# Sums of squares of the norms: two rounded parts in place of one fp32 product

## The chip, the cores and the metric

The kernel runs on one core of one Trainium2 chip. The metric is the device time of one execution in microseconds (us); lower is better. A core has five engines that run their own instruction queues and meet at semaphores: PE (TensorE, matmuls, with its weight loads shown apart as PEld), DVE (VectorE), ACT (ScalarE), POOL (GpSimd) and SP (SyncE, which issues most DMAs). Matmuls read operands from SBUF and write PSUM; POOL reads and writes SBUF alone.

## The reference

Three blocks follow each other on 512 tokens of width 1024: layer 0 (16 meta tokens are put in front, so 528 rows; a gated linear recurrence "hgrn2" with 4 heads beside latent attention "mla" with 4 heads, then an MLP), layer 1 (a pooling mixer and an MLP), and a second block (sparse attention with 8 heads, a gated linear attention "gla" with 4 heads, then a mixture of 32 experts). What the change touches are norms inside the first and the last of them:

```python
def rmsnorm(x, g):
    xf = x.astype(jnp.float32)
    y = xf * lax.rsqrt(jnp.mean(xf * xf, axis=-1, keepdims=True) + EPS)
    return (y * g.astype(jnp.float32)).astype(x.dtype)

# layer 0: per head of the recurrence (128 wide), per latent (256 wide), per key (192 wide)
o = rmsnorm(o, out_gain) * jax.nn.silu(hg...)
q = jnp.einsum('blr,re->ble', rmsnorm(cq, qa_g), w_q_up)...
kv = jnp.einsum('blr,re->ble', rmsnorm(ckv, kva_g), w_kv_up)...
k = rope_tail(rmsnorm(k, kn_g), cos, sin)
# second block: queries and keys per head of 64, gla output per head of 128
qa = rmsnorm_2(qa.reshape(bsz, s_len, A_HEADS, A_HEAD_DIM), q_norm_g[l])
ka = rmsnorm_2(ka.reshape(bsz, s_len, A_HEADS, A_HEAD_DIM), k_norm_g[l])
o_b = rmsnorm_2(o_b, gla_out_norm_g[l])...
```

## The kernel before

The state is kept transposed: features lie on the 128 partitions, tokens along the free axis, so the residual `h` is eight tiles of 128 x 528 (512 in the second block). Every dense product is made exact enough by splitting both operands into a rounded high part and the remainder (type fp32r) and multiplying three times: high x high, high x low, low x high (`dense`, L289; `mm3`, L266 to L268). ACT rounds (L259) and DVE subtracts (L260); SP streams the raw weights in half megabyte pieces (L253).

A norm over features is a sum over partitions. `ones_sum` (L478) makes it on PE: a constant matrix (`self.ones`, or `self.blk` with two blocks of 64) is the stationary operand, the tile of squares is streamed, both as plain fp32, and every row of the result holds the sum. In layer 0 a result of 528 columns is two halves of 264 in a pair of PSUM banks (L485); in the second block it is one product of 512 columns (L489). `rstd_rows` (L472) then takes Ln (L475) and Exp (L476) on ACT, and DVE multiplies. The squares come from ACT (Square) right before: L810 for a head of the recurrence, L848 for a latent, L942 with an addition at L943 for a key, L1973 for a gla head, L2005 for an attention projection. A latent is 256 wide, two tiles, so its sum has two operands in `pairs`.

Scratch tiles of 528 columns come from a ring of ten places (`tmp`, pool `t`); the second block has a ring of seven places of 512 columns besides (`gtmp`, pool `b2t`). A tile holds its place until its last reader is done, and places go to tiles in the program's order.

The order of the work is written as weaves: generators (`hgrn_head`, `mla_up`, `dsa_proj`, `gla_heads` and others) that yield between pieces are interleaved by `WEAVES` in layer 0 and `WEAVES_2` in the second block. On top of that a planner orders each engine's queue by readiness, with the program's order as priority. In layer 0 the first weave ends with the second latent (`B1`) and its norm; then PSUM is divided anew (`banks(2, 4)`), a mask is loaded through POOL (L634) and the second weave begins with the first head (L569). In the second block the first weave makes the eight attention projections (`dsa_proj`) beside the index products (`index_tile`, Relu at L1820, six scratch places held by their operands); each projection's sum is called behind the next projection's Square, the last one's at the end. Top-k runs on DVE (L1836, L1837) pinned to the program's order. `gla_gate` (L1863) loads a small weight `w2` through POOL (L1867) into a tile of its own and multiplies it at L1873; `rel_bias` fills the ring of seven with its tables and uses them at L1759 and L1774.

## Time and profile before

| | us |
|---|---|
| median of 3 runs | 1750.56 |
| lowest, highest | 1749.06, 1750.74 |
| the profiled execution | 1750.7 |
| its span, first to last instruction | 1748.8 |
| busy: PE, DVE, ACT, POOL | 1700.9, 1090.7, 860.5, 54.5 |
| mean granted clock of PE, share of full speed | 0.987 |

The page gives, for one execution, busy time by engine, the chain of work that ended last, and groups of instructions. Matmuls are pipelined and their ends are modelled, so that records of PE overlap: the mean duration of a record is longer than the step from one to the next, and the chain in order of time is where the step is seen. A releaser behind "<-" is the instruction that ended a wait.

### The profile page before, as it was taken

The numbers are of one execution on the slowest core, as the hardware profiler recorded it, in microseconds if no ns is written. First come the engines' busy times: TensorE is split into PE (matmuls) and PEld (weight loads), VectorE is DVE, ScalarE is ACT, GpSimd is POOL, SyncE is SP. The second block draws the span as 40 slices with busy tenths as digits, with TensorE's granted clock in tenths as the row PEclk, the third lists the DMA queues.
The fourth block names the chain that finished last, engine by engine and source line by source line (L and its number), as shares of the span: only waits on it lengthen the run. The fifth ranks groups of instructions, "written<-read, shape, count | busy, mean of one in ns | idle before, by whom it ended". The sixth has DMA issues, their size and how long they took to land.

```text
span 1748.8 us, 26901 instructions
## 1 busy us (share of the span) xinstructions
PE 1700.9 (97%) x10674; PEld 1494.4 (85%) x10674; DVE 1090.7 (62%) x1885; ACT 860.5 (49%) x1419; POOL 54.5 (3%) x66
## 2 busy tenths in 40 slices
PE   8999999999999999999999999999999999999996
PEld 7999999999999999878888888767767788888884
DVE  7677675643434344553434345589867768999996
ACT  5456654432323133541413134454346359999995
POOL 0000000000000000000000000100000000101111
PEclk9999999999999999999999999999989999999999
DMA  5211113332323232133333334322201468999994
GB/s 190 70 50 49 37 37 106 85 96 86 94 88 94 89 91 79 61 91 93 94 97 96 96 97 135 111 73 73 73 13 55 160 224 292 348 339 377 374 375 136
DMA packets 72482, 228.42 MB, mean 131 GB/s; under 512 B 8456, under 2 KB 8512, under 8 KB 72352
## 3 DMA queue, kind: packets, MB, share of 16 engines
q1 hardware_dynamic: 69120, 216.22, 36.4%
q0 software_dynamic: 3232, 10.44, 3.0%
q8 instruction: 85, 1.39, 0.3%
q14 instruction: 45, 0.37, 0.1%
HBM read 213.50 MB, written 13.12 MB: 130 GB/s over the span
## 4 chain that ended last, share of the span: by engine, by line
PE 92%; DVE 5%; ACT 2%; issue 1%; DMA 0%; SPq 0%; POOL 0%; POOLq 0%; DVEq 0%; ACTq 0%
PE pm L289 32%; PE ps L289 29%; PE ps L1591 7%; PE ps L1571 3%; PE ps L266 3%; PE ps L267 2%; PE ps L268 2%; PE ps L557 2%; PE ps L2062 1%; DVE wlo L260 1%; PE ps L2037 1%; PE ps L1192 1%; PE pm L485 1%; PE ps L2055 1%; DVE acc L1837 1%
## 5 line engine op out<-in xcount | busy, mean ns | idle before, releaser
L259 ACT CAST whi<-wraw 128x1024 fp32r<-128x1024 f32 (+1 forms) x309 | 321.3, 1045 | 606.6 <-PE pm L289 293.1
L260 DVE TENSOR_TENSOR wlo<-wraw,whi 128x1024 fp32r<-128x1024 f32 (+1 forms) x309 | 373.4, 1217 | 42.5 <-ACT whi L259 32.3
L289 PE MATMUL pm<-xh,whi 128*128 128x264 f32 x976 | 202.2, 288 | 8.7 <-ACT whi L259 5.9
L289 PE MATMUL pm<-xh,wlo 128*128 128x264 f32 x976 | 200.9, 287 | 0.5 <-DVE wlo L260 0.5
L289 PE MATMUL pm<-xl,whi 128*128 128x264 f32 x976 | 200.6, 287 | 0.0
L289 PE MATMUL ps<-xh,whi 128*128 128x512 f32 x472 | 192.1, 407 | 0.0
L289 PE MATMUL ps<-xh,wlo 128*128 128x512 f32 x472 | 186.2, 395 | 0.0
L289 PE MATMUL ps<-xl,whi 128*128 128x512 f32 x472 | 185.5, 393 | 0.0
L289 PEld LDWEIGHTS pm<-xh,whi 128*128 128x128 f32 x976 | 152.8, 190 | 9.8 <-ACT whi L259 5.9
L289 PEld LDWEIGHTS pm<-xh,wlo 128*128 128x128 f32 x976 | 152.7, 190 | 0.8 <-DVE wlo L260 0.7
L289 PEld LDWEIGHTS pm<-xl,whi 128*128 128x128 f32 x976 | 152.2, 189 | 0.4 <-DVE xl L467 0.3
L289 PEld LDWEIGHTS ps<-xh,whi 128*128 128x128 f32 x472 | 89.3, 189 | 23.6 <-issue 1.8
L289 PEld LDWEIGHTS ps<-xh,wlo 128*128 128x128 f32 x472 | 89.1, 189 | 21.0
L289 PEld LDWEIGHTS ps<-xl,whi 128*128 128x128 f32 x472 | 89.3, 189 | 19.4 <-issue 0.5
L1591 PE MATMUL ps<-wlo,xg 128*128 128x512 f32 x256 | 103.8, 406 | 1.7 <-DVE wlo L260 1.6
L289 PE MATMUL pm<-ah,whi 128*128 128x264 f32 x512 | 104.2, 285 | 0.0
L289 PE MATMUL pm<-ah,wlo 128*128 128x264 f32 x512 | 104.0, 285 | 0.0
L1591 PE MATMUL ps<-whi,xg 128*128 128x512 f32 x256 | 103.7, 405 | 0.0
L289 PE MATMUL pm<-al,whi 128*128 128x264 f32 x512 | 103.7, 284 | 0.0
L289 PE MATMUL ps<-ah,whi 128*128 128x512 f32 x256 | 101.1, 395 | 0.0
L289 PE MATMUL ps<-ah,wlo 128*128 128x512 f32 x256 | 101.0, 394 | 0.0
L289 PE MATMUL ps<-al,whi 128*128 128x512 f32 x256 | 100.5, 393 | 0.0
(501 smaller groups left out, 3202.4 us busy)
## 6 DMA issues: line engine op xcount, KB each, us to landing
wraw<-in_stream_dram SPq DMA_DIRECT2D x306, 512.0 KB, 3.6
t<-in_stream_dram SPq DMA_DIRECT2D x90, 256.0 KB, 6.9
h<-in_stream_dram SPq DMA_DIRECT2D x37, 512.0 KB, 6.0
h<-in_xT_dram SPq DMA_DIRECT2D x16, 264.0 KB, 4.3
hd<-h SPq DMA_DIRECT2D x8, 256.0 KB, 2.0
h<-hd SPq DMA_DIRECT2D x8, 256.0 KB, 4.2
out_dram<-t SPq DMA_DIRECT2D x8, 256.0 KB, 2.3
gt<-rbd POOLq DMA_DIRECT2D x4, 256.0 KB, 5.6
```

The source lines that it names most:

```text
L259: self.nc.scalar.copy(hi, src)
L260: i = self.nc.vector.tensor_sub(lo, src, hi.bitcast(F32))
L266: nc.tensor.matmul(ps, wh, xh, start=start, stop=False)
L267: nc.tensor.matmul(ps, wh, xl, start=False, stop=False)
L268: nc.tensor.matmul(ps, wl, xh, start=False, stop=stop)
L289: nc.tensor.matmul(ps, w[:, b, :], x[:, sl], start=(first and f and i == 0), stop=(last and l and i == nb - 1))
L485: nc.tensor.matmul(pm[:, s, :H2], l, r[:, s * H2:(s + 1) * H2], start=i == 0, stop=i == len(pairs) - 1)
L557: nc.tensor.matmul(pa[:, j * 64:(j + 1) * 64], xs, self.second(xs, i), start=True, stop=True)
L1192: nc.tensor.matmul(ps[:, i * 128:i * 128 + n], self.z[:, i, cols], self.bands[i][:, g, :n], start=False, stop=i == NT - 1, skip_group_chec ...
L1571: nc.tensor.matmul(pg[:, j * m:(j + 1) * m], src[2 * i + k // 4][:, sl], oh[:, i, :m], start=i == 0, stop=i == NT - 1, skip_group_check=True)
L1591: nc.tensor.matmul(pa, xk, v[:, k], start=kk == 0 and n == 0, stop=kk == 7 and n == 1, skip_group_check=True)
L1837: nc.vector.match_replace(out=acc, in_to_replace=m8, in_values=acc, imm_value=sel)
```

## The change

`ones_sum` takes one constant and a tuple of operands. A new helper `parts` makes that tuple: ACT copies the squares into a rounded tile, POOL subtracts it from the squares for the remainder. The constants `ones` and `blk` are copied once into a rounded tile `c2` by DVE. All sums that go through `ones_sum` are then two rounded products of the same constant. For a latent, POOL first adds the two tiles of squares, so that its sum has one tile too. The gate's weight `w2` moves from a tile of its own into the ring of seven. The sums that use one column of `self.ones` (L427, L926) stay as they are.

```diff
--- before.py
+++ after.py
@@ -475,9 +475,17 @@
         nc.scalar.activation(out, ps, AF.Ln, scale=1.0 / dim, bias=self.epsb)
         nc.scalar.activation(out, out, AF.Exp, scale=-0.5)
 
-    def ones_sum(self, pairs, n=T):
-
-        nc = self.nc
+    def parts(self, x, n=T):
+
+        hi, lo = (self.p_t.tile([128, T], F32R, name="t")[:, :n] for _ in range(2))
+        self.nc.scalar.copy(hi, x)
+        self.nc.gpsimd.tensor_sub(lo, x, hi.bitcast(F32))
+        return hi, lo
+
+    def ones_sum(self, l, x, n=T):
+
+        nc = self.nc
+        pairs = [(l, r) for r in x]
         if n == T:
             pm = self.pm()
             for s in range(2):
@@ -583,6 +591,9 @@
 
         xh, xl = self.xsplit(h, "mix0", first=first)
         nc.sync.dma_start(self.c128, self.a["c128"].rearrange("p (a b) -> p a b", a=4))
+        c2 = self.p_c.tile([128, 2, 128], F32R, name="c2")
+        nc.vector.tensor_copy(c2, self.c128[:, 1:3])
+        self.onesr, self.blkr = c2[:, 0], c2[:, 1]
         self.rb2 = None
         self.o = h
         with ExitStack() as es:
@@ -808,9 +819,10 @@
 
         sq = self.tmp()
         nc.scalar.activation(sq, o, AF.Square)
+        sq = self.parts(sq)
         yield
         yield
-        pn = self.ones_sum([(self.ones, sq)])
+        pn = self.ones_sum(self.onesr, sq)
         ro = self.tmp()
         self.rstd_rows(self.v2(ro), pn, 128)
         while "g" not in st:
@@ -828,7 +840,7 @@
         lat = [([], []), ([], [])]
 
         def norm(which, gname):
-            pn = self.ones_sum([(self.ones, sqs[which, 0]), (self.ones, sqs[which, 1])])
+            pn = self.ones_sum(self.onesr, sqs[which, 2])
             r = self.tmp()
             self.rstd_rows(self.v2(r), pn, 256)
             for j in range(2):
@@ -848,6 +860,8 @@
             nc.scalar.activation(sq, z, AF.Square)
             zs[which, j], sqs[which, j] = z, sq
             if j == 1:
+                nc.gpsimd.tensor_add(sq, sq, sqs[which, 0])
+                sqs[which, 2] = self.parts(sq)
                 return lambda: norm(which, gname)
 
         def keys(pm):
@@ -944,8 +958,10 @@
             krr[h] = p1.tile([128, T], F32, name=("lh00", "lh01", "ll00", "ll01")[h])
             nc.gpsimd.memset(krr[h], 0.0)
 
+            sn = self.parts(sn)
+
             def norm():
-                pn = self.ones_sum([(self.ones, sn)])
+                pn = self.ones_sum(self.onesr, sn)
                 f = self.tmp()
                 self.rstd_rows(self.v2(f), pn, 192)
                 nc.vector.scalar_tensor_tensor(k, k, gg, f, op0=OP.mult, op1=OP.mult)
@@ -1863,7 +1879,7 @@
     def gla_gate(self, p, comb):
 
         nc = self.nc
-        w2 = p.tile([64, 256], F32, name="w2")
+        w2 = self.gtmp(256)
         nc.gpsimd.dma_start(w2[32:48], self.a["gate_w2"])
         gb = p.tile([128, 2], F32, name="gb")
         nc.gpsimd.dma_start(gb, self.a["gate_b"])
@@ -1971,12 +1987,12 @@
             nc.scalar.copy(o, pos[par])
             sq = self.gtmp(S)
             nc.scalar.activation(sq, o, AF.Square)
-            os.append((o, sq))
+            os.append((o, self.parts(sq, S)))
         yield
         for par in range(2):
             h = 2 * f + par
             o, sq = os[par]
-            pn = self.ones_sum([(self.ones, sq)], S)
+            pn = self.ones_sum(self.onesr, sq, S)
             ro = self.gtmp(S)
             n = 0
             while "g" not in gate[h]:
@@ -2003,11 +2019,12 @@
                 nc.vector.tensor_mul(z, pm, rb)
                 sq = self.tmp(S)
                 nc.scalar.activation(sq, z, AF.Square)
+                sq = self.parts(sq, S)
                 if late:
                     late()
 
                 def late(z=z, sq=sq, g=g):
-                    pn = self.ones_sum([(self.blk, sq)], S)
+                    pn = self.ones_sum(self.blkr, sq, S)
                     r = self.tmp(S)
                     self.rstd_rows(r, pn, 64)
                     nc.vector.scalar_tensor_tensor(z, z, g, r, op0=OP.mult, op1=OP.mult)
```

## Rows read from the trace of the kernel before

**Rows 1.** The page: its first line and section 4, the chain by engine.

```profile
span 1748.8 us, 26901 instructions
PE 92%; DVE 5%; ACT 2%; issue 1%; DMA 0%; SPq 0%; POOL 0%; POOLq 0%; DVEq 0%; ACTq 0%
```

**Rows 2.** Groups on PE: line, shapes, count, busy us, mean ns, idle before.

```profile
L485 PE MATMUL pm<-t,c 128*128 128x264 f32 x48 | 12.5, 391 | 1.0 <-ACT t L848 1.0
L489 PE MATMUL ps<-t,c 128*128 128x512 f32 x16 | 8.3, 598 | 0.6 <-ACT t L2005 0.6
L489 PE MATMUL ps<-gt,c 128*128 128x512 f32 x8 | 3.9, 592 | 0.0
```

**Rows 3.** The chain in order of time: start us, length us, what, count.

```profile
52.69 1.78 PE pm L485 x8
231.95 2.94 PE pm L289 x24
1384.86 1.72 PE ps L489 x4
1389.60 5.55 PE ps L289 x24
```

**Rows 4.** Groups on ACT, POOL and DVE (columns as in rows 2).

```profile
L259 ACT CAST lh<-t 128x528 fp32r<-128x528 f32 x4 | 2.4, 628 | 0.8 <-DVE t L836 0.8
L945 POOL MEMSET ll<- 128x528 f32 x2 | 1.1, 536 | 9.5 <-PE pm L289 9.5
L635 DVE CAST msk<-t 128x384 uint8<-128x384 f32 x1 | 0.4, 358 | 0.0
```

**Rows 5.** Timeline, 64 to 68 us: start, length, instruction, idle before and its releaser.

```profile
64.00 0.64 ACT L848 ACTIVATE t<-t 128x528 f32<-128x528 f32 x1
66.34 0.70 ACT L475 ACTIVATE t<-pm,epsb 128x528 f32<-128x528 f32 x1 [1.69 <-PE pm L485]
64.70 1.60 PE L485 MATMUL pm<-t,c 128*128 128x264 f32 x6 [1.03 <-ACT t L848]
67.09 1.16 PE L569 MATMUL ps<-q,kk 128*128 128x128 f32 x8 [0.79 <-ACT t L475]
```

**Rows 6.** Stretches: busy us (instructions) of PE, PEld, DVE, ACT, POOL; PE clock; DMA.

```profile
120.00:140.00 20.00, 20.00 (x123) 17.25 (x122) 11.05 (x19) 15.42 (x29) 0.20 (x1) 1.00 0.15 48
180.00:190.00 10.00, 8.41 (x66) 7.70 (x65) 6.30 (x19) 7.32 (x18) 0.20 (x1) 1.00 0.17 55
1115.00:1182.00 67.00, 66.41 (x286) 44.32 (x286) 52.76 (x112) 35.91 (x63) 3.43 (x5) 1.00 0.28 87
```

**Rows 7.** The chain by line, 1176 to 1211 us.

```profile
by line: DVE acc L1837 26.6%; DVE m L1836 22.7%; DVE wlo L260 12.9%; issue 9.6%; DVE gt L534 4.0%; DVE gt L535 4.0%; DVE gb L1883 3.4%; DVE gt L1880 3.4%; DVE dqa L2013 2.1%; DVE gt L1881 2.1%; DVE dka L2013 1.9%; ACT t L476 1.8%; DVE gt L1
```

**Rows 8.** Timeline of ACT and PE around one attention projection's sum.

```profile
1127.33 0.63 ACT L2005 ACTIVATE t<-dka 128x512 f32<-128x512 f32 x1
1134.42 1.02 PE L489 MATMUL ps<-t,c 128*128 128x512 f32 x2
```

**Rows 9.** The views of single lines: duration ns min/median/max, first and last start us.

```profile
L1759 PE MATMUL ps<-gt,rbt x2: 481/482/484, 1112.1 to 1112.5; 32*8 32x384 f32 x2
L1774 PE MATMUL ps<-gt x8: 592/593/593, 1176.2 to 1179.2; 128*128 128x512 f32 x8
L1867 POOL DMA_DIRECT2D w<-in_gate_w_dram x1: 505/505/505, 1096.2 to 1096.2; - x1
L1873 PE MATMUL ps<-comb,w x4: 587/588/692, 1179.7 to 1181.1; 16*128 16x512 f32 x4
```

**Rows 10.** Timeline of POOL, the mask's load.

```profile
54.63 0.60 POOL L634 DMA_DIRECT2D t<-in_msk_dram  x1 [51.62 <-PE pm L485]
```

**Rows 11.** Timeline of POOL and DVE, 1488 to 1492 us.

```profile
1488.63 2.25 POOL L1496 DMA_INDIRECT out_dram<-y,sr  x1 [16.79 <-ACT xg L1573]
1489.80 1.22 DVE L260 TENSOR_TENSOR wlo<-h,whi 128x1024 fp32r<-128x1024 f32 x1 [0.35 <-ACT whi L259]
1491.14 1.21 DVE L260 TENSOR_TENSOR wlo<-wraw,whi 128x1024 fp32r<-128x1024 f32 x1
```

## Prediction

> **What bounds the kernel now.** I read the views in this order: the page's chain of work, the groups of the sums of squares on the matrix engine, the same sums in the chain in order of time, and then a timeline wherever a sum's inputs come from just ahead of it.
>
> The chain that ended last is PE for 92% of the span [rows 1]. So what PE executes counts one to one wherever PE is packed, and what ACT, DVE or POOL execute counts only where PE, or what PE feeds, waits for it. The sums to be changed are three groups: 48 matmul records of 264 columns at L485 and 16 + 8 records of 512 columns at L489 [rows 2]. An fp32 product leaves two records, so these are 24 products in ten sums (four heads, four keys, two latents with two squares each), two halves a sum, and 12 products in twelve sums of block 2 (eight attention projections, four gated heads).
>
> The mean duration of a record is not its price, since matmuls overlap. The chain in order of time has the price: eight fp32 records in 1.78 us, 0.2225 each, and four of 512 columns in 1.72 us, 0.43 each. The projections around them multiply rounded (fp32r) operands: 24 records of 264 columns in 2.94 us, 0.1225 each, and 24 of 512 in 5.55 us, 0.231 each [rows 3]. A rounded record costs a little over half of an fp32 record, and a rounded product is one record where an fp32 product is two.
>
> **The change part by part.**
>
> Removed from PE: 48 x 0.2225 = 10.7 us and 24 x 0.43 = 10.3 us, together 21.0. Added: every sum is now two rounded products (high and low part) of full width, and the latents' two squares are added first, so ten sums x 2 halves x 2 = 40 x 0.1225 = 4.9 us, and twelve x 2 = 24 x 0.231 = 5.5 us. Net 10.6 us off PE, if every sum stood where PE is packed.
>
> Added ahead of each sum: one ACT copy that rounds (a row of the same shape: 0.63 us) and one POOL subtraction; for each latent norm a POOL addition besides. That is 22 copies (13.9 us of ACT) and 24 POOL operations. The trace has no POOL operation that reads tiles. Its nearest row is a POOL memset of the same 128x528: 0.536 us for one stream written [rows 4]. Three streams, overlapped or one behind the other, lie between 0.54 and 1.6 us; nothing below, since an operation is added and none goes. I take the middle, 1.1 us, and keep both ends. The Trainium skill (GPSIMD Engine Reference, section Elementwise — side-by-side cycle accounting) gives 4497 ns for an addition over 2048 columns, from which 528 columns would be an estimated 1.16 us; by it the latents' term below grows by 0.1 us.
>
> So a sum's inputs come about 0.63 + 1.1 + two hand-overs of 0.06 (Square's end at 64.64 to the matmul at 64.70 [rows 5]) = 1.85 us later, and some sums give up what they gain.
>
> *The second latent's norm.* It is the last thing of the first weave. Its Square ends at 64.64, PE waits for it, six records run, Ln starts at 66.34, and the next PE work (L569) waits for that Ln before it starts at 67.09 [rows 5]; DVE's and PE's next stage stand behind that. From Square to Ln now: 1.70 us. After: 1.1 (add) + 0.63 (copy) + 1.1 (subtract) + 4 x 0.06 + 4 x 0.1225 + 0.31 (last record to Ln, as now: 1.64 - 6 x 0.2225) = 3.87 us. The stage starts 2.2 us later, and the 1.29 us that this sum's records were credited with above are not gained: a loss of 3.5 us against the credit. With POOL's ends it is 2.4 to 4.5; it is 0 if PE finds projection work to do meanwhile, which it did not find in the 0.79 us ahead of L569.
>
> *A head's norm at 185 us.* PE is busy only 8.41 of the 10 us around it, ACT 7.32 [rows 6]. The 0.4 us that the sum saves fills idle time, and the 0.63 us copy queues on ACT ahead of the softmax exponentials that this stretch waits for. Loss 0.7, between 0.4 and 1.0.
>
> *The last two attention sums, 1173.6 to 1176.* From 1176 to 1211 the chain is DVE's top-k steps (L1836, L1837: 49%) [rows 7], so the 0.8 us that PE saves in these two sums returns nothing. The last sum's chain grows, but top-k steps of two blocks are at hand to fill DVE; a POOL subtraction that held DVE up would cost up to 1.1 there. I take 0.8 + 0.5, between 0.8 and 2.4.
>
> *The other sums* I take as covered. In the attention stretch a Square ends at 1127.96 and its sum starts at 1134.42 [rows 8]: 6.5 us of projection matmuls cover 1.85. Among the keys, 120 to 140 us, PE is busy 20.0 of 20 [rows 6], with the values' matmuls as cover; ACT's 15.4 us there grow by about five copies, 3.2 us, and stay under 20. If that cover were gone, a key would cost 1.85 less the 0.4 saved.
>
> *Edits with one answer.* The copy of two constant blocks is one DVE instruction of 256 columns; a conversion of 384 takes 0.36 us [rows 4]. The first sum comes at 52 us, so it lies beside other work: 0, or 0.36 on DVE's path to the first matmul. The gate's weight moves into a ring of seven buffers. Six others and the one-hot table fill the ring, so its load, issued at 1096.2 now, waits for the table's release after L1759, read at 1112; on POOL's queue the bias store and loads follow it. It is read at 1179.7 [rows 9], so some 65 us cover it: 0. Only if it got the buffers that L1774 reads until 1179 would PE wait some 4 us.
>
> The sum: 10.6 - 3.5 - 0.7 - 1.3 = 5.1 us. The profiled execution took 1750.7 us around a span of 1748.8, which is also the runs' median (1750.56) within 0.2. Forecast: 1745.6 us.
>
> **The rivals.**
>
> *All of it returns.* PE has other work at the latents' end, and the chains are covered: 1750.7 - 10.6 = 1740.1. For it: the planner may order PE's work anew. Against: the two waits in rows 5.
>
> *The buffers run out.* The ring of scratch tiles has ten places, and each sum now takes two more of them until it has run. The ring is short already: the mask's load on POOL, ready from the start, waited 51.6 us, until the first latent's sum gave a place back [rows 10]. In the attention projections six of the ten places hold the index operands; the high and low parts hold two more through the following projection, so the index products' Relu and the next Square would wait for places. If each of the eight projections lost 0.6 us of the 1.85 to this, that is 5 us: 1750.5, no change.
>
> *POOL holds DVE up.* Slower. If a POOL operation that reads two tiles keeps a DVE operation with two tile inputs waiting to its end, DVE loses up to 24 x 1.1 = 26 us, where it is busy 52.8 of 67 us [rows 6], and it makes the low halves of the weights that PE needs. Half of that on the path is 13 us, less the 0.5 already taken: 1745.6 + 12.5 = 1758. It decides from 0.2 us an operation (5.1 / 24). Against it, as far as rows go: beside POOL's 2.25 us scatter a DVE subtraction took 1.22 us, and right after it one of the same shape 1.21 [rows 11]; but that POOL instruction reads no tile to compute. The Trainium skill (SBUF — State Buffer, section SBUF: two separate sides) says just this, that the two engines share a pair of ports under an exclusive lock, and that a DVE operation with two inputs in SBUF and a GpSimd operation that reads SBUF block each other for a whole instruction. By that rule this rival's mechanism is certain and only its share on the path is open; no row here has the pair, so the trace neither agrees nor differs.
>
> *It does not do what it says.* The rounded products with the new constant run at the fp32 record's price: 40 x 0.2225 + 24 x 0.43 = 19.2, only 1.8 us off, and the delays of about 4 us remain (2.2, 0.7 and 1.3): some 1753. Against it: all rounded rows show the lower price.
>
> **How the numbers follow.** 0.2%, or 3.5 us, is about what a measurement of this kernel can tell from no change; faster ends at 1747.1, slower begins at 1754.1. The forecast case has 0.50, with a range of its own of 1743 to 1748.5 (the bounds of its terms): 0.41 faster, 0.09 the same. All of it returns: 0.14, faster. Buffers run out: 0.16, the same. POOL holds DVE up: 0.15, slower. Not what it says: 0.05, the same. So faster 0.55, same 0.30, slower 0.15. The range reaches from the full gain to the fp32-priced case, 1740 to 1753; it leaves out the slower rival and little else.
>
> **What would show it.** Right: 40 records at L485's successor at about 0.12 us in the chain and 24 at 0.23; POOL subtractions near 1.1 us; L569's start some 2 us later against the end of the B1 projection; heads, keys and attention sums without a wait ahead of them on PE. Wrong: DVE instructions of unchanged shape that last longer, or start late, beside POOL's; Relu or Square in the attention stretch waiting for a sum.

## The result and the profile after

| | before | after |
|---|---|---|
| median, us | 1749.8 | 1777.6 |
| lowest, highest, us | 1748.2, 1750.7 | 1777.2, 1779.0 |
| the profiled execution, its span, us | 1750.7, 1748.8 | 1777.3, 1775.6 |
| PE's mean granted clock | 0.987 | 0.978 |

The changed kernel takes 1.0161 times the time of the kernel before (95% interval 1.0144 to 1.0179): 28 us more, where 5 less were forecast and the range ended at 1753. The page's chain of the changed kernel breaks off at its last instruction, an output transfer on POOL, so nothing here rests on it. Its groups by line, which answer [rows 2, 4] (columns as there; L493 and L497 are the sums, L481 the rounding copy, L482 the subtraction, L863 the addition of a latent's squares):

```profile
L493 PE MATMUL pm<-t,c 128*128 128x264 f32 x40 | 10.3, 355 | 14.9 <-POOL t L482 6.5 <-ACT t L481 5.1 <-DVE ll L968 3.3
L497 PE MATMUL ps<-t,c 128*128 128x512 f32 x24 | 10.1, 480 | 6.4 <-ACT t L481 4.5 <-POOL t L482 1.9
L481 ACT CAST t<-t 128x528 fp32r<-128x528 f32 x10 | 6.3, 634 | 4.5 <-POOL t L863 3.7 <-DVE t L957 0.6
L481 ACT CAST t<-t 128x512 fp32r<-128x512 f32 x8 | 5.0, 621 | 0.3
L482 POOL TENSOR_TENSOR t<-t 128x528 fp32r<-128x528 f32 x10 | 15.5, 1550 | 77.8 <-ACT t L481 72.1 <-PE ps L268 3.4 <-issue 2.3
L482 POOL TENSOR_TENSOR t<-t 128x512 fp32r<-128x512 f32 x8 | 10.3, 1290 | 46.6 <-ACT t L481 40.2 <-DVE wlo L260 6.4
L863 POOL TENSOR_TENSOR t<-t 128x528 f32<-128x528 f32 x2 | 3.5, 1760 | 59.4 <-ACT t L860 59.4
```

The counts are the forecast ones, 40 and 24 records. What was not forecast stands behind the second bar: PE is idle 14.9 and 6.4 us ahead of its sums, where it was 1.0 and 0.6 before [rows 2].

Where the time went is read by taking the same PE instruction in both traces, by its first start, and subtracting. Lines are those of the kernel before; the first column is its time there, the others how much later (us) the same work starts. The other kernels are those of the experiments.

| place (line before) | before | after | sub_on_dve | keys_as_before | parts_unread | layer0_only | block2_only |
|---|---|---|---|---|---|---|---|
| behind the latents (L569) | 67.1 | 5.0 | 1.5 | 4.7 | 0.3 | 4.8 | 0.0 |
| sums of the queries (L926) | 106.5 | 7.6 | 4.5 | 7.5 | 0.2 | 6.3 | 0.1 |
| behind the keys (L1020) | 143.9 | 17.5 | 12.2 | 8.2 | 2.5 | 18.1 | 0.0 |
| behind the second head's norm (L1066) | 208.9 | 21.0 | 12.7 | 11.2 | 3.4 | 20.2 | 0.1 |
| second block begins (L1799) | 1111.8 | 20.8 | 13.7 | 11.2 | 3.7 | 21.0 | 1.2 |
| last attention sums (L1774) | 1176.2 | 23.0 | 13.5 | 13.4 | 7.9 | 21.1 | 4.0 |
| attention begins (L2037) | 1206.8 | 25.7 | 16.2 | 15.8 | 9.9 | 21.1 | 6.7 |
| behind the gated heads (L1369) | 1442.5 | 26.9 | 14.0 | 16.0 | 9.7 | 21.3 | 7.5 |

So four places lose: the latents (7.6 until PE runs evenly again), the keys (9.9), the norm of the recurrence's second head, at 185 us in the kernel before (3.5), and the end of the attention projections (4.9). The gated heads add 1.2. In `parts_unread` and `layer0_only` some 1.5 us of the row "behind the keys" are not the keys': there the clock fell behind a pause near 112 us (119 in `layer0_only`), ahead of the keys' sums, and in the changed kernel it did not (last section).

*The latents.* Timeline of the changed kernel, which answers [rows 5] (start, length, instruction, idle before and its releaser):

```profile
65.49 0.65 ACT L860 ACTIVATE t<-t 128x528 f32<-128x528 f32 x1
66.21 1.75 POOL L863 TENSOR_TENSOR t<-t 128x528 f32<-128x528 f32 x1 [10.71 <-ACT t L860]
66.72 1.78 DVE L755 TENSOR_TENSOR t<-c,b 128x512 f32<-128x512 f32 x1
67.99 0.63 ACT L481 CAST t<-t 128x528 fp32r<-128x528 f32 x1 [1.86 <-POOL t L863]
68.67 0.59 PE L493 MATMUL pm<-t,c 128*128 128x264 f32 x1 [3.97 <-ACT t L481]
68.70 1.48 POOL L482 TENSOR_TENSOR t<-t 128x528 fp32r<-128x528 f32 x1 [0.74 <-ACT t L481]
68.91 1.56 DVE L543 TENSOR_TENSOR t<-b 128x264 f32<-128x264 f32 x1
70.24 1.03 PE L493 MATMUL pm<-t,c 128*128 128x264 f32 x3 [0.97 <-POOL t L482]
71.30 0.70 ACT L475 ACTIVATE t<-pm,epsb 128x528 f32<-128x528 f32 x1 [2.68 <-PE pm L493]
72.05 2.08 PE L577 MATMUL ps<-q,kk 128*128 128x128 f32 x8 [0.79 <-ACT t L475]
```

From Square's end to Ln it is 71.30 - 66.14 = 5.16 us instead of 1.70. PE waits 3.97 and 0.97 us, and its next work (L577, L569 before) takes 2.08 us where it took 1.16 [rows 5]: the clock has fallen.

*The clock.* Stretches of the changed kernel, columns as in [rows 6]; the last four figures are POOL, PE's granted clock, DMA share, GB/s:

```profile
66.00:78.00 12.00, 7.56 (x32) 6.95 (x33) 8.45 (x13) 4.25 (x8) 3.76 (x3) 0.57 0.18 60
148.00:160.00 12.00, 7.27 (x34) 6.90 (x33) 7.23 (x15) 5.86 (x11) 2.25 (x1) 0.57 0.28 89
203.00:212.00 9.00, 7.95 (x40) 7.54 (x40) 3.38 (x13) 4.16 (x12) 0.10 (x1) 0.62 0.01 2
1196.00:1206.00 10.00, 7.44 (x12) 3.38 (x13) 6.55 (x16) 5.82 (x10) 1.28 (x1) 0.66 0.17 52
```

In each of the four places the clock falls to 0.5, the 1.2 GHz level, after PE has waited. The kernel before ran these places at 1.00. By the means, PE lost 7.56 x 0.43 + 7.27 x 0.43 + 7.95 x 0.38 + 7.44 x 0.34 = 11.9 us there, an estimate, since a mean covers the pauses too. It is on the high side: at the latents it gives 3.3, and what PE falls behind there after the norm is 2.6 (5.0 to 7.6).

So of the 27 us by which the span grew, the idle time ahead of the sums is 19.7 (21.3 less 1.6) and the clock some 12, less the 10.6 of saved work; the 6 that are left are not divided further; other pauses are among them, such as 2.6 us at the softmax beside the second head's norm, where it was 1.4.

*The keys.* The changed kernel's timeline of ACT and POOL for the third and fourth key, with one line of DVE (a weight's subtraction) and one of PE (the fourth key's sum); L956 is a key's Square, L475 Ln:

```profile
142.90 0.70 ACT L475 ACTIVATE t<-pm,epsb 128x528 f32<-128x528 f32 x1 [0.47 <-PE pm L493]
143.50 0.64 ACT L956 ACTIVATE t<-kn 128x528 f32<-128x528 f32 x1
145.04 0.64 ACT L481 CAST t<-t 128x528 fp32r<-128x528 f32 x1
145.76 1.72 POOL L482 TENSOR_TENSOR t<-t 128x528 fp32r<-128x528 f32 x1 [3.65 <-ACT t L481]
148.22 0.70 ACT L475 ACTIVATE t<-pm,epsb 128x528 f32<-128x528 f32 x1 [1.12 <-PE pm L493]
148.81 0.63 ACT L956 ACTIVATE t<-kn 128x528 f32<-128x528 f32 x1
150.81 0.63 ACT L481 CAST t<-t 128x528 fp32r<-128x528 f32 x1
151.40 1.21 DVE L260 TENSOR_TENSOR wlo<-wraw,whi 128x1024 fp32r<-128x1024 f32 x1
151.50 0.59 PE L493 MATMUL pm<-t,c 128*128 128x264 f32 x1 [3.32 <-DVE ll L968]
151.52 2.25 POOL L482 TENSOR_TENSOR t<-t 128x528 fp32r<-128x528 f32 x1 [4.04 <-ACT t L481]
154.89 0.70 ACT L475 ACTIVATE t<-pm,epsb 128x528 f32<-128x528 f32 x1 [3.44 <-PE pm L493]
```

On ACT a key's Square stands behind the Ln of the key before. So copy, subtraction and sum lie in a loop from key to key: 5.3 and 6.7 us from Ln to Ln. Before, the same order of ACT's queue gave 130.83, 134.11 and 137.39, 3.3 us each. How much of the loss is this loop is asked by `square_first` below.

*The second head's norm.* Timeline of POOL, DVE and PE in the changed kernel (L509 multiplies two tiles in SBUF, L1001 is the maximum that the softmax waits for, L1027 the next attention scores), then the same multiplication and scores in the kernel before:

```profile
201.42 1.68 POOL L482 TENSOR_TENSOR t<-t 128x528 fp32r<-128x528 f32 x1 [2.25 <-issue]
201.86 1.80 DVE L509 TENSOR_TENSOR q<-t 128x528 f32<-128x528 f32 x1
203.66 0.41 DVE L1001 TENSOR_REDUCE mx<-pm 128x1 f32<-128x272 f32 x1
205.03 0.82 PE L1027 MATMUL pm<-kn,qn 128*128 128x136 f32 x2 [1.01 <-ACT t L1007]
```

```profile
184.49 0.70 DVE L501 TENSOR_TENSOR q<-t 128x528 f32<-128x528 f32 x1
186.55 0.50 PE L1011 MATMUL pm<-kn,qn 128*128 128x136 f32 x2 [0.18 <-ACT t L991]
```

Beside POOL's subtraction the multiplication takes 1.80 us instead of 0.70; the maximum behind it on DVE comes later, so do the softmax and PE, which waits 1.01 us instead of 0.18. An earlier pause (1.59 instead of 1.22) has the copy in ACT's queue ahead of the softmax. Then the clock falls. With the subtraction on DVE (`sub_on_dve`) the multiplication takes 0.71, the second pause is 0.39, the clock stays at 1.00 and the place loses 0.5 us instead of 3.5.

*The attention projections.* Timeline of the changed kernel around one of them (L2021 Square, L1836 an index product's Relu, L476 the Exp of the norm before, L2030 its multiplication on DVE):

```profile
1148.17 0.63 ACT L2021 ACTIVATE t<-dka 128x512 f32<-128x512 f32 x1
1148.84 0.62 ACT L481 CAST t<-t 128x512 fp32r<-128x512 f32 x1
1149.37 0.68 ACT L475 ACTIVATE t<-ps,epsb 128x512 f32<-128x512 f32 x1
1149.60 1.30 POOL L482 TENSOR_TENSOR t<-t 128x512 fp32r<-128x512 f32 x1 [5.33 <-ACT t L481]
1150.93 0.38 ACT L1836 ACTIVATE t<-ps 128x256 f32<-128x256 f32 x1 [0.88 <-POOL t L482]
1151.21 0.62 ACT L476 ACTIVATE t<-t 128x512 f32<-128x512 f32 x1
1151.87 0.75 DVE L2030 SCALAR_TENSOR_TENSOR dqa<-dqa,qg,t 128x512 f32<-128x512 f32 x1
```

The Relu waits until POOL has read the squares: it needs their place in the ring. Exp stands behind the Relu, and behind Exp the DVE work that comes ahead of the next projection's multiplication. How far that multiplication (L2003 before) starts behind the sum that PE runs at the projection's end, second to eighth projection, in us:

| kernel | 2 | 3 | 4 | 5 | 6 | 7 | 8 |
|---|---|---|---|---|---|---|---|
| before | 0.2 | 0.2 | 0.2 | 0.2 | 0.2 | 0.2 | 0.2 |
| after | 0.2 | 0.2 | 1.6 | 2.9 | 3.7 | 4.2 | 4.2 |
| block2_only | 0.2 | 0.5 | 1.3 | 2.6 | 3.4 | 4.1 | 4.2 |
| parts_unread | 0.2 | 0.2 | 1.2 | 2.1 | 2.5 | 3.0 | 3.4 |
| block2_copy_on_pool | 0.2 | 0.7 | 1.4 | 3.2 | 4.2 | 5.3 | 4.1 |
| block2_relu_psum | 0.2 | 0.2 | 0.6 | 1.1 | 1.8 | 2.3 | 2.6 |
| block2_both | 0.2 | 0.2 | 0.4 | 0.5 | 0.5 | 0.6 | 1.0 |

While projections follow, PE has other work and the lag costs nothing. Behind the last one it has none: it waits 4.45 us for the last sum (1194.10 to 1198.56), and the fourth stretch at half clock follows.

### The profile page after: what moved, and what is told of

It reads as the page before. It is cut to its first block, busy times and chain, and to the rows that moved or that the text cites. A ratio compares the mean times of both kernels' runs of the same rounds, so it can differ in the third digit from the quotient of the medians.

```text
span 1775.6 us, 26964 instructions
## 1 busy us (share of the span) xinstructions
PE 1703.9 (96%) x10666; PEld 1499.4 (84%) x10666; DVE 1094.3 (62%) x1886; ACT 873.5 (49%) x1441; POOL 89.5 (5%) x90
## 5 line engine op out<-in xcount | busy, mean ns | idle before, releaser
L260 DVE TENSOR_TENSOR wlo<-wraw,whi 128x1024 fp32r<-128x1024 f32 (+1 forms) x309 | 373.5, 1217 | 41.5 <-ACT whi L259 31.4
```

The source lines that it names most:

```text
L260: i = self.nc.vector.tensor_sub(lo, src, hi.bitcast(F32))
```

## The experiments

Every run stands beside runs of the kernel before on its own chip (medians 1749.8 to 1753.1), so the ratio is what is compared. The kernel before itself took 1747.1 to 1755.0 us in them, at granted clocks from 0.988 down to 0.984, so that a difference of a few microseconds between single traces can be the clock's alone.

**Who subtracts, and which half.** Four kernels. `sub_on_dve`:

```diff
-        self.nc.gpsimd.tensor_sub(lo, x, hi.bitcast(F32))
+        self.nc.vector.tensor_sub(lo, x, hi.bitcast(F32))
...
-                nc.gpsimd.tensor_add(sq, sq, sqs[which, 0])
+                nc.vector.tensor_add(sq, sq, sqs[which, 0])
```

> The changed kernel with the 22 subtractions and the latents' two additions on DVE instead of POOL. In the changed kernel's trace the POOL subtraction takes 1.28 to 2.25 us and the latents' addition 1.76; DVE's subtraction of the same shape takes 0.70. Theory A (PE's order is fixed, so every microsecond that a sum's inputs come later is waited for on PE, and a wait of several microseconds is followed by a granted clock of 0.5): the pause of 3.97 us ahead of the second latent's sum shrinks by about 1 us of addition and 0.6 to 1.5 of subtraction, each key by 0.6 to 1.5, but the rounding copy and a DVE step remain: 1757 to 1767. Theory B (POOL holds DVE, and that alone is the loss): no POOL operation reads tiles any more, so the forecast's gain appears: 1742 to 1750. Theory C (what costs is the copies and the new place of the sums in the queues, whoever subtracts): 1772 or more.

Measured: 1764.3, ratio 1.0079 (1.0062 to 1.0096), as theory A says. Half of the loss goes with POOL, half stays: the second head's norm loses 0.5 us instead of 3.5, the keys still lose 7.7, and the longest pause ahead of a key's sum is even longer, here (PE's sums, timeline):

```profile
142.68 0.64 PE L493 MATMUL pm<-t,c 128*128 128x264 f32 x3 [0.95 <-DVE t L482]
148.25 0.59 PE L493 MATMUL pm<-t,c 128*128 128x264 f32 x1 [4.94 <-ACT t L481]
```

`layer0_only`, with the fp32 sum put back in block 2:

```diff
-            os.append((o, self.parts(sq, S)))
+            os.append((o, (sq,)))
...
-            pn = self.ones_sum(self.onesr, sq, S)
+            pn = self.ones_sum(self.ones, sq, S)
...
-                sq = self.parts(sq, S)
+                sq = (sq,)
...
-                    pn = self.ones_sum(self.blkr, sq, S)
+                    pn = self.ones_sum(self.blk, sq, S)
```

> The change in layer 0 alone; the sums of block 2 are one fp32 product as before (the gate's weight stays in the ring of seven). In the changed kernel L1799, the first landmark of block 2, stands 20.8 us later than before, and the end 26.8. Theory A with the losses local to each place: 1750 + 21 = 1771. If instead the block 2 loss follows from layer 0 (a shifted transfer), block 2's landmarks move on here too, to 1776.

`block2_only`, the same for the latents, heads and keys of layer 0 (the latents' two squares are two products again):

> The change in block 2 alone (attention projections and gated heads); layer 0's sums are one fp32 product as before. Local losses: the last attention sums +5 and the end of the gated heads +1, so 1750 + 6 = 1756, with the 4.5 us pause on PE ahead of the last attention sum and the stretch at clock 0.5 after it as in the changed kernel. If layer 0 is what disturbs block 2: 1745 to 1750, the 2.5 us by which the six covered sums are shorter.

Measured: 1773.9, ratio 1.0133 (1.0116 to 1.0150), and 1756.9, ratio 1.0035 (1.0020 to 1.0049). The excess over 1, 1.33% and 0.35%, adds up to 1.68% against 1.61%: the losses are local, as expected. `layer0_only` took a time between its two forecasts, 1771 and 1776, but its trace stays at 21 us through the second block.

`parts_unread`, in which copies and subtractions are made and nothing reads them:

```diff
-        return hi, lo
+        return (x,)
...
-                nc.gpsimd.tensor_add(sq, sq, sqs[which, 0])
-                sqs[which, 2] = self.parts(sq)
+                s2 = self.tmp()
+                nc.gpsimd.tensor_add(s2, sq, sqs[which, 0])
+                self.parts(s2)
...
-            pn = self.ones_sum(self.onesr, sqs[which, 2])
+            pn = self.ones_sum(self.ones, (sqs[which, 0], sqs[which, 1]))
```

> All 22 rounding copies on ACT, all 24 POOL operations (the latents' sums of squares into a tile of their own) are made at the same places, but nothing reads them: the sums are fp32 products of the squares as before. So PE waits for no copy and no subtraction, while ACT, POOL and DVE do what they do in the changed kernel. Theory A: what is lost is the waiting of the sums, so 1750 to 1755. Theory B: DVE is held by POOL all the same, so most of the 27 us remains: 1765 or more.

Measured: 1760.3, ratio 1.0054 (1.0037 to 1.0071), between the two. In layer 0 theory A holds: 0.3 us is lost at the latents and 2.3 from the queries' sums to behind the keys, 1.5 of them at half clock ahead of the first key's sum, so nearly all of the loss at the latents and the keys is waiting for the parts. At the second head's norm 0.9 is lost: DVE's multiplication takes 1.82 us beside POOL there too, but the clock did not fall behind it. In the attention stretch theory A falls: 6.2 us are lost although no sum reads a part, and a Relu waits for POOL there as in the changed kernel (the waits between 1130 and 1190 us: engine, line, releaser, us in total, times, longest):

```profile
ACT t L1837 <- POOL t L482: 2.6, 3, 0.9
```

**Is it the keys?** `keys_as_before`:

```diff
-            sn = self.parts(sn)
+            sn = (sn,)
...
-                pn = self.ones_sum(self.onesr, sn)
+                pn = self.ones_sum(self.ones, sn)
```

> The changed kernel with the four keys' sums of layer 0 as one fp32 product again; latents, heads and block 2 stay changed. In the changed kernel the lateness grows by 9.9 us between the last query sum and the first attention scores (7.6 to 17.5). If the keys' own chain (copy and subtraction in a loop from key to key) is what costs there: 9 to 10 us come back, 1767 to 1769. If POOL and ACT work of the heads and the shifted transfers do it: less than 5 us.

Measured: 1767.5, ratio 1.0092 (1.0075 to 1.0109). From the queries' sums to behind the keys it loses 0.7 us instead of 9.9. `square_first` asks for the loop itself, by the order of tracing in `dense_seq`:

```diff
+                if last:
+                    new = done(acc if j == 0 else acc[0])
                 if j == 0 and late:
                     late()
                     late = None
                 if last:
-                    late = done(acc if j == 0 else acc[0])
+                    late = new
```

> The changed kernel with one order of tracing turned round: in layer 0's short projections (keys and queries) the finish of a key, with its Square and its parts, is put ahead of the norm of the key before. In the changed kernel ACT's order is Ln of one key, then Square of the next, so the new copy and subtraction lie in a chain from key to key: 5.3 and 6.7 us from Ln to Ln against 3.3 before. If that chain is what the keys lose: two Squares stand ahead of a Ln, half of the hand-overs go, and 4 to 6 of the keys' 10 us come back, 1771 to 1774. If each key waits only for its own parts: no gain, 1776 or more.

Measured: 1773.7, ratio 1.0116 (1.0099 to 1.0133). In its trace the keys lose 7.9 us instead of 9.9, and the end is 3.7 us earlier than in the changed kernel. So the order in ACT's queue is 2.0 of the 9.9 us, where 4 to 6 were expected, and most of the loss is there without it. Keys are tied together elsewhere too: in the changed kernel PE's weight load for the third key's product waits for a Ln (138.43 us), which reads a pair of PSUM banks. Whether that tie, or the longer chain of each single key, is the larger part of the rest was not tested.

**What is the saving on PE worth alone?** `high_only` takes every added step away and leaves the low part of the squares out, so its sums are those of the rounded squares. The edit of a recurrence head's square; the others are alike:

```diff
-        sq = self.tmp()
+        sq = self.p_t.tile([128, T], F32R, name="t")
         nc.scalar.activation(sq, o, AF.Square)
-        sq = self.parts(sq)
+        sq = (sq,)
```

> Every sum is one rounded product per square: Square on ACT writes the rounded square itself, so there is no copy, no subtraction and no addition, and the low part of the squares is left out (the sums are those of the rounded squares; the latents' two squares are two products). What is left of the change is PE's saving alone: 48 x 0.2225 + 24 x 0.43 = 21.0 us go, 24 x 0.1225 + 12 x 0.231 = 5.7 come, 15.3 net. Theory A (the loss is the added latency and the added work in the queues of ACT, POOL and DVE): it all goes, and most of the saving shows, 1735 to 1742. Rival (PE's saving is given back wherever PE waits next): within 4 us of the kernel before.

Measured: 1748.4 beside 1753.1, ratio 0.9984 (0.9966 to 1.0001): no difference that can be told. Its profiled execution is one of its longest (1756.5), because the half clock after one pause near 1276 us lasted longer, so only its start is read. It gains 2.3 us at the latents (of 2 x (1.78 - 4 x 0.1225) = 2.6 saved). Behind the pause near 112 us the clock falls in this trace (0.66 in the mean from 111 to 116 us) and not in the kernel before, and 1.6 of it are gone again. From there to behind the keys 1.8 come, for four keys and a head's sum among them (of 5 x (0.89 - 2 x 0.1225) = 3.2), and 3.3 in the attention projections (of 8 x (0.86 - 0.231) = 5.0). At the last key PE now waits (timeline of PE):

```profile
136.52 0.48 PE L493 MATMUL pm<-t,c 128*128 128x264 f32 x2 [0.71 <-DVE t L955]
138.22 0.51 PE L289 MATMUL pm<-xh,whi 128*128 128x264 f32 x2 [0.37 <-ACT t L475]
```

So where PE was full, a shorter sum does return time, 7.4 of 10.8 us in these three places, but not one to one: the chain through ACT and DVE takes a part, 1.1 us in these two waits. Over the whole program hardly any of it shows. The granted clock is one reason: the ten runs have 0.976 to 0.986, the kernel before beside them 0.984 to 0.987. Why it is lower is not shown.

**What lowers the clock?** `warm` puts products ahead of two sums, into the bank that the sum overwrites:

```diff
+            for _ in range(reps):
+                for s in range(2):
+                    nc.tensor.matmul(pm[:, s, :H2], self.ones, fill[:, s * H2:(s + 1) * H2], start=True, stop=True)
             for s in range(2):
...
-            pn = self.ones_sum(self.onesr, sqs[which, 2])
+            pn = self.ones_sum(self.onesr, sqs[which, 2], fill=sqs[which, 0], reps=4 * which)
...
-                pn = self.ones_sum(self.onesr, sn)
+                pn = self.ones_sum(self.onesr, sn, fill=k, reps=3 if h == 3 else 0)
```

> The changed kernel with work for PE in its two longest pauses of layer 0: ahead of the second latent's sum four fp32 products of the first latent square, and ahead of the last key's sum three of the key itself, into the bank that the sum then overwrites (8 and 6 matmuls, some 3.6 and 2.7 us, into pauses of 3.97 and 3.32 us). No wait is taken away. In the changed kernel the granted clock is 0.5 from 68 to 77 and from 150 to 159 us, and PE is busy at it for some 7 us in each, which costs half of that. If the pauses are what lowers the clock: both stretches run at 1.0 and the time falls by 5 to 7 us, to 1771 to 1773. If the clock falls for another reason, or the products only delay the sums: 1777 to 1780.

`warm2` fills all three pauses around the second latent's sum (`full` is the sum's pair of banks, `other` a bank that nobody reads, `fill` the first latent's square; `half` takes 264 columns and `pin` keeps the program's order):

```diff
...
+                for i in range(9):
+                    mm(full[:, i % 2, :H2], self.ones, half(fill, i % 2), start=True, stop=True)
+                pin(mm(full[:, 0, :H2], self.onesr, half(hi, 0), start=True, stop=False))
+                for i in range(3):
+                    pin(mm(other[:, :H2], self.ones, half(fill, i % 2), start=True, stop=True))
+                pin(mm(full[:, 0, :H2], self.onesr, half(lo, 0), start=False, stop=True))
...
+                for i in range(2):
+                    pin(mm(other[:, :H2], self.ones, half(fill, i % 2), start=True, stop=True))
```

> The changed kernel with PE kept busy through all three pauses around the second latent's sum: nine fp32 products of the first latent square ahead of it (some 4.0 us, into the bank that the sum overwrites), three between its first high product and its first low one (1.3 us) and two behind it (0.9 us), into a bank that nobody reads. With products ahead of the sum alone, pauses of 0.42, 1.16 and 0.79 us were left within 3.4 us, and the granted clock fell to 0.5 all the same from 71 us on. If the pauses lower it: the clock stays at 1.0 from 62 to 80 us, and from the attention scores behind this norm (L577) to the first products of the next weave nothing is lost (2.6 us in the changed kernel), 1774 to 1776. If it falls with hardly a pause left: the cause is another.

Measured: 1775.2, ratio 1.0127 (1.0108 to 1.0146), which fits neither expectation, and 1774.8, ratio 1.0121 (1.0107 to 1.0136). Stretches of `warm`, then of `warm2` (columns as above):

```profile
62.00:71.00 9.00, 7.08 (x41) 5.79 (x39) 5.60 (x6) 2.57 (x4) 3.81 (x3) 1.00 0.28 87
71.00:77.00 6.00, 5.55 (x25) 5.56 (x26) 3.98 (x8) 3.18 (x6) 0.00 (x0) 0.51 0.13 36
```

```profile
62.00:80.00 18.00, 18.00 (x123) 16.34 (x122) 10.96 (x16) 5.96 (x10) 3.79 (x3) 1.00 0.18 56
```

With some 2 us of pauses left the clock fell; with PE busy 18.00 of 18 us it stayed at 1.00. The second latent's norm then cost 3.1 us (from 2.9 late ahead of it to 6.0 at the queries' sums), where it costs 6.1 in the changed kernel (1.5 to 7.6). So the pauses are what lowers the clock here, as far as one trace of each can show it. The norm's own chain stayed long, 4.77 us from Square to Ln (5.16 in the changed kernel): filled pauses save only what the clock took.

The trace of `warm2` also has the other side. At the first latent's norm, where nothing was filled, PE waits 1.08 and 0.75 us in both kernels. In the changed kernel the clock stayed at 1.00 behind that; in `warm2` it fell, which cost 1.4 us (stretch of `warm2`, columns as above):

```profile
56.00:60.00 4.00, 4.00 (x23) 4.00 (x22) 1.45 (x2) 1.98 (x3) 0.00 (x0) 0.57 0.02 6
```

**Why does the multiplication lag?** The first idea, the copy in ACT's queue, was tried with `block2_copy_on_pool` (on `block2_only`):

```diff
-        self.nc.scalar.copy(hi, x)
+        self.nc.gpsimd.tensor_copy(hi, x)
```

> The change in block 2 alone, with the rounding copy on POOL as well, ahead of the subtraction, instead of on ACT. In the kernel with the change in block 2 alone DVE's multiplication that ends a projection comes 0.2 us after the next sum's start in the first round and 4.2 in the last, because ACT does a copy of 0.62 us between Square and the Ln of the sum before, and DVE's order has that norm and three top-k rounds ahead of the next multiplication. If the copy in ACT's queue is the cause: the lag stays under 1.5 us, 1746 to 1751. If it is the two more places that each sum takes of the ring of ten (they are held longer here), or POOL beside DVE (there is more of it here): 1757 or more.

Measured: 1761.9, ratio 1.0051 (1.0034 to 1.0068). The idea falls: the lag grows to 5.3 us, and the Relu waits longer (timeline of ACT); 1.6 us of the time are not block 2's, but half clock near 112 us:

```profile
1149.29 0.49 ACT L1834 ACTIVATE t<-ps 128x384 f32<-128x384 f32 x1 [2.01 <-POOL t L482]
1149.68 0.62 ACT L476 ACTIVATE t<-t 128x512 f32<-128x512 f32 x1
```

`block2_relu_psum` and, with the kernel before, `before_relu_psum` take the Relus out of the ring:

```diff
-            r = self.tmp(n)
-            nc.scalar.activation(r, ps[:, :n], AF.Relu)
+            r = ps[:, :n]
+            nc.scalar.activation(r, ps[:, :n], AF.Relu)
```

> The change in block 2 alone, and the index products' Relu writes its result back over its bank in PSUM instead of into a place of the ring of ten, so the Relus ask for no place. In the kernel with the change in block 2 alone a Relu waits 0.86 us for the end of POOL's subtraction (with the copy on POOL too, 2.0), and the Exp of the sum before stands behind it on ACT; DVE's multiplication then comes 4.2 us after the sum's start in the last round (0.2 before). If the ring's places are the cause of block 2's loss: no Relu waits for POOL, the lag stays at 0.2 to 1.5 us, and the time is at most that of the kernel before with the same Relu, less up to 4 us. If the longer way to the sum itself is the cause: the lag and the pause of 4.4 us ahead of the last attention sum remain, and it is 5 us or more above that kernel.

> The kernel before with the index products' Relu in PSUM, as a measure for the run beside it: its sums are fp32 products as they were. No Relu waited for a place in the kernel before, so within 4 us of it; a bank is held longer by each Relu and read by DVE in PSUM, which may cost up to 3.

Measured: 1757.0, ratio 1.0029 (1.0019 to 1.0040), and 1749.8, ratio 1.0001 (0.9989 to 1.0013). The Relu in PSUM costs nothing by itself, no Relu waits for POOL any more, and the lag falls from 4.2 to 2.6 us: between the two expectations. The stretch from L1799 to L2037 loses 2.4 us instead of the 5.5 of `block2_only`. `block2_both` has both edits:

> The change in block 2 alone, with the Relus in PSUM and the rounding copy on POOL: no Relu asks for a place of the ring, and no copy stands in ACT's queue between Square and the Ln of the sum before. DVE's multiplication stood 4.2 us behind the sum's start in the last round with the change in block 2 alone, 5.3 with the copy on POOL alone (a Relu then waited up to 2.0 us for a place), and 2.6 with the Relus in PSUM alone (the copy was still in ACT's queue). If the places and the copy are the two causes: the lag is under 1 us in the last round, the pause ahead of the last attention sum is under 3 us, and the time is 1748 to 1753. If the lag comes from POOL's work itself (2.4 us of it a sum now, beside DVE): 2 us of lag or more, and 1756 or more.

Measured: 1755.9, ratio 1.0026 (1.0015 to 1.0038). The lag is 1.0 us at most, the stretch from L1799 to L2037 loses 1.6 us, and up to the last sums (L1774) the stretch runs 0.8 us ahead of the kernel before. So places and copy together make the lag: with the places short, taking the copy off ACT was worse; with places enough, it took the lag from 2.6 to 1.0. The time stays above the forecast's 1753, because the last sum has no cover however short the lag: PE still waits 3.08 us for it, the clock falls behind that (2.3 us more by L2037), and 3.0 go in the gated heads.

**What is left.** `best` keeps the two parts only where cover was shown, in the first six attention projections, with both aids:

```diff
-                sq = self.parts(sq, S)
+                sq = self.parts(sq, S) if j < 3 else (sq,)
...
-                def late(z=z, sq=sq, g=g):
-                    pn = self.ones_sum(self.blkr, sq, S)
+                def late(z=z, sq=sq, g=g, l=self.blkr if j < 3 else self.blk):
+                    pn = self.ones_sum(l, sq, S)
```

> Only the first six attention projections sum in two parts, with the copy and the subtraction on POOL and the Relus in PSUM; the last two, the gated heads and all of layer 0 are one fp32 product as before. In the kernel with the change in all of block 2 and these two aids, the attention stretch up to the last sums ran 0.8 us ahead of the kernel before, and the rest of its loss came with the pause of 3.1 us ahead of the last sum (2.3 with the clock behind it) and with the gated heads (3.1). Without these: 6 x (0.86 - 0.46) = 2.4 us less than before at most, 1748 to 1750, not to be told from no change; if the pause ahead of the last sums comes back: 1753.

Measured: 1747.2 beside 1752.7, ratio 0.9979 (0.9966 to 0.9993): 0.2% faster than the kernel before. Its trace has 1.8 us of it at the last attention sums, of 2.4 saved; another 2.2 us come near 1300 us, where the sums are as before and the half clock behind a pause at 1277 us lasted 14 us instead of 17, so that part isn't the edit's own. The runs overlap (1746.4 to 1756.0 beside 1747.1 to 1755.0), and only 1.8 us have a cause that is shown.

## Why the prediction was wrong

- *PE's prices* were right (at full clock two 512-column records step by 0.23 us and two of 264 by 0.12, and counts as forecast). But "what PE executes counts one to one wherever PE is packed" held in part only: `high_only` got back 2.3 of 2.6 us at the latents, 1.8 of 3.2 at the keys, where PE was busy 20.0 of 20 [rows 6], and 3.3 of 5.0 in the attention projections. It took 15.3 us from PE in all, and the median moved by 4.7.
- *POOL's price* was nearly right: 1.1 taken between 0.54 and 1.6, 1.27 to 1.35 measured where nothing disturbs it. The mean of 1.55 in layer 0 has waiting for DVE in it.
- *The second latent's norm*: the place and the mechanism were right, the size was not. From Square to Ln 5.16 us against 3.87 forecast (POOL's two operations 3.2 against 2.2, and the low product's records at half clock); the first latent's norm, which the sum treated as covered, had cost 1.5 us already (pauses of 1.08 and 0.75); and the clock took another 2.6. Forecast: a start 2.2 us later; measured 5.0, then 7.6.
- *The step that failed most* is "The other sums I take as covered", and in it the keys: no loss was forecast and 0.4 us of gain a sum, measured was a loss of 9.9, of which 9.2 go with the keys' own parts (`keys_as_before`). It judged cover by PE's busy share of the stretch. But PE works in its queue's order, and a sum whose parts come late holds up what stands behind it (`parts_unread`: 0.7 us at the keys when no sum reads its parts). The longer way to a sum is paid at every key. The order of ACT's queue, where a key's Square stands behind the Ln of the key before, is 2.0 us of it (`square_first`); how the rest divides is open. The text even had the price of a key without cover, 1.85 less 0.4; four of them make 5.8, and the clock behind them is some 3.1 more by the estimate above.
- *A head's norm at 185 us*: 0.7 forecast, 3.5 measured. It was lost where PE waits for the softmax, as the term had it (two pauses, 1.6 and 1.0 us). The copy in ACT's queue, the term's only delay, goes with the first; the second comes from POOL holding DVE, and the clock falls behind them.
- *The last attention sums*: 1.3 forecast (0.8 to 2.4) against a credit of 0.4 for each of the eight sums, so a stretch that ends 1.9 us earlier; it ended 4.9 later, because the lag of DVE's multiplication had grown to 4.2 us by then. It is the mechanism of the rival *The buffers run out*: Relus waiting for a sum's places, priced at 5 us over eight projections. Block 2 alone loses 5.5 between L1799 and L2037. Without the Relus in the ring 2.4 of that are left. The loss does not come at each projection, as the rival had it, but behind the last. It was put as the whole story at 1750.5 and was a part of it.
- *The clock* was no term at all. By the estimate above it is some 12 of the 27 us, or a little less. The forecast counted a pause of PE at its own length.
- *The rival POOL holds DVE up* had the slower side and a mechanism that happens (below). On the path it was at the second head's norm, 3.0 of the 3.5 us by `sub_on_dve`, the clock behind it included. As the main cause it fails: `parts_unread` has all of POOL's work and loses 0.3 us at the latents and 0.7 at the keys. The 13 us between the last row of `after` and that of `sub_on_dve` are 3.0 there, 3.1 at the latents and 2.2 at the keys, where PE waits for POOL's results, and most of the rest in block 2; that rest is not divided further.
- *The gate's weight* was rightly taken at 0 (`layer0_only` has it in the ring and stays at 21.0 to 21.3 us through the second block), and *It does not do what it says* was rightly set aside.

## What to carry to other kernels

A full engine is no proof of cover. Before a step is added ahead of an in-order engine's operand, follow what stands behind the consumer, on that engine and in the queues of the others: where the next round's first step waits there, a part of the step is paid every round. Count each new pause of PE with the half-clock stretch that may follow it; here that was of the same order as the pauses. And where a step holds scratch places longer, look for the instruction that asks for a place next, and for what is queued behind that one.

## What the runs showed of the hardware that was not expected

POOL and DVE do wait for one another, and it depends on the operands. In the timeline of the latents above, DVE's L755 (two inputs in SBUF) takes 1.78 us beside POOL's addition instead of 0.68, ending 0.5 us behind it, and L543 takes 1.56 beside the subtraction instead of 0.43; L509 at the second head's norm takes 1.80 instead of 0.70. POOL waits as well: the last key's subtraction took 2.25 us, behind a DVE subtraction (L260) that had started 0.12 us earlier and ended 1.16 us before it. A DVE operation of 128x512 with one input in PSUM (L579) ran inside a POOL subtraction (145.76 to 147.48 us) and took 0.69 us, as in the kernel before. One line of the kernel before (L744 there is L755 now) and one of the changed kernel, timelines of DVE:

```profile
65.24 0.68 DVE L744 TENSOR_TENSOR t<-c,b 128x512 f32<-128x512 f32 x1
146.35 0.69 DVE L579 TENSOR_TENSOR at<-ps,c 128x512 f32<-128x512 f32 x1
```

The Trainium skill (SBUF — State Buffer, section SBUF: two separate sides) has this rule; the trace agrees with it. Over the 24 POOL operations, DVE's instructions that overlap them were some 5.6 us longer in sum than the median of the same line and shape in the same trace.

The clock does not always fall after the same pause. A pause of 1.15 us near 112 us, ahead of the perm product (L876), left the clock at 1.00 in the kernel before and was followed by some 4 us at 0.5 in five of the other traces: `parts_unread`, `high_only`, `layer0_only`, `block2_copy_on_pool` and `block2_relu_psum`. In the last two that stretch is the same code as before. The first latent's pauses in `warm2` are another case, and so are the two at the second head's norm, 1.59 and 1.01 us in the changed kernel, where the clock fell, and 1.59 and 0.94 in `parts_unread`, where it did not. What decides there stays open.
